# Squares and roots of the second norm issued with the residual, and a broadcast PSUM column as the scan's unused second operand

## Chip, cores, metric

One core of a Trainium2 chip. The metric is the time of one execution of the program in microseconds (us); the time of a kernel is the median of its runs. A profile is one further execution, recorded instruction by instruction.

## What is computed

One layer of a streaming encoder in float32, for a prompt of 2048 frames and a sample of 32 frames with 2048 cached frames. Cut to what matters here:

```python
x = x + rmsnorm(mixer(rmsnorm(x, g_mix_pre)), g_mix_post)   # mixer: stick-breaking attention | SSD, one output projection
x = x + rmsnorm(conv_ffn(rmsnorm(x, g_ffn_pre)), g_ffn_post)

# stick-breaking attention: 8 heads of 64, strictly causal
z = einsum('bqhd,bkhd->bhqk', q, k) * 64 ** -0.5
log_keep  = where(causal, log_sigmoid(-z), 0)
log_after = cumsum(log_keep, reverse=True) - log_keep
w = where(causal, exp(log_sigmoid(z) + log_after), 0)
out = einsum('bhqk,bkhd->bqhd', w, v)
```

The kernel computes `w` without logarithms: beta = sigmoid(z), gam = sigmoid(-z), a running product of gam from the right (a scan), and beta times that product.

## The kernel before

The frames are worked through in four blocks of 512 (the last one of 544, with the sample in it). For each block there are two streams of work.

- **Attention** (`Attention.heads`). Block s has 32 (s + 1) slots, one for 128 queries of one head against 512 keys: 320 slots in all, and 10 more for the sample. A slot is: two score matmuls into the PSUM tile `z` (lines 801 and 805; two buffers, so slot i writes the buffer of slot i-2), two sigmoids on ScalarE (line 652 `beta`, line 656 `gam`), the scan on VectorE into `prow` (line 659), the product (line 664, four of five on GpSimd, one of five on VectorE), four transposes on TensorE into `pt` (line 822), a copy to `wt` (line 825), and after every fourth slot the product with the values into `pa` (line 837). The loop issues the scores of slot i, then some of the other stream (`fill`), then the transposes of slot i-2 (`LOOK = 2`).
- **The rest of the layer** (`Tail.stream`) for the block before, which runs as a generator between the slots. Its matmuls are split into three passes each and go through the helper `dense` (line 124), which fixes their order against the attention's matmuls. In order: the first part of what the block before left over (`owed`, the last two groups of its down projection); the output projection of both halves a and b of the block (`out_units`); `residual(a)`, stepped along with the projection of half b; `residual(b)`; `split` of both halves (`xhi`, `xlo`, the two parts of the next matmuls' input); the rest of `owed`; `root` of both halves; then, for each of 22 units j, `up` (a gate matmul into bank `o`, multiplied by the root `r` on line 984, and an up matmul into bank `u`), and `down` per group of units. The last block's stream runs with no attention beside it.

`residual` takes the root of the mixer's squares (`rstd_narrow`), scales `m`, loads x (DMA, line 930), adds it (line 935, four of eight on GpSimd, four on VectorE), and stores the sum (DMA, line 936). `root` squares that sum, eight pieces per half, and takes the second norm's root `r`. The squares go through one buffer:

```python
    def square(self, sq, x, first):
        if first:
            nc.scalar.activation(sq, x, AF.Square)                         # line 758
        else:
            t = self.tmp.tile([P, 272], F32, name="sqt")[:, : sq.shape[-1]]  # one buffer
            nc.scalar.activation(t, x, AF.Square)                          # line 761
            nc.gpsimd.tensor_tensor(sq, sq, t, op=ALU.add)                 # line 762
```

Each `rstd_narrow` sums the squares with small matmuls into PSUM (line 166), takes the power on VectorE and GpSimd (lines 176 and 184), spreads the result with four small matmuls (line 195) and copies it out on ScalarE (line 201). While attention runs, its two PSUM tiles are taken from the single buffer of bank `u`, which is also that of the up matmuls; tiles of one buffer are handed on in the order in which the program asks for them.

The order of instructions on each engine is fixed at compile time by a planner that takes them roughly in the program's order as it expects them to become ready; on the chip each engine works through its list in order.

Of the kernel before, what the change touches and what calls it, by code (L numbers as in the profile page):

```python
# [23 lines left out]
P = 128  # L24
# [33 lines left out]
def tiles_of(n):  # L58
    return [(0, n)] if n <= 512 else [(0, n // 2), (n // 2, n)]
# [549 lines left out]
class Attention:  # L609
# [38 lines left out]
    def weights_of(self, z, n, prev):  # L648

        nc = self.kn.nc  # L650
        b = self.bp.tile([P, 512], F32, name="beta", bufs=4)
        nc.scalar.activation(b[:, :n], z, AF.Sigmoid, scale=0.125)  # L652
        self.n += 1
        g = self.gam[self.n % 3]
        c0 = 512 - n
        nc.scalar.activation(g[:, c0:512], z, AF.Sigmoid, scale=-0.125)  # L656
        pr = self.pp.tile([P, 513], F32, name="prow", bufs=5)
        back = lambda t: t[:, c0:513][:, ::-1]
        nc.vector.tensor_tensor_scan(  # L659
            back(pr), back(g), back(g), self.kn.ones[:, 0:1] if prev is None else prev,  # L660
            op0=ALU.mult, op1=ALU.bypass,
        )
        eng = nc.vector if self.n % MUL_DVE == 1 else nc.gpsimd
        eng.tensor_tensor(b[:, :n], b[:, :n], pr[:, c0 + 1 : 513], op=ALU.mult)  # L664
        return b, pr[:, c0 : c0 + 1]
# [204 lines left out]
class Tail:  # L870
# [48 lines left out]
    def residual(self, s, half):  # L919

        kn, nc, att = self.kn, self.kn.nc, self.att
        t0 = SBS[s][0]
        c0, c1 = half
        n = c1 - c0
        rm = att.tmp.tile([P, 272], F32, name="rstd")
        kn.rstd_narrow(att.tmp, *kn.bank, [self.msq[:, c0:c1]], n, D, out=rm)
        yield
        for c, m in enumerate(self.m):
            x = (self.late or att.tmp).tile([P, 272], F32, name="xr", bufs=8 if self.late else 2)
            nc.sync.dma_start(x[:, :n], kn.a["xT"][:, c, t0 + c0 : t0 + c1])  # L930
            nc.vector.scalar_tensor_tensor(
                m[:, c0:c1], m[:, c0:c1], kn.col(C_GMIXP + c), rm[:, :n], op0=ALU.mult, op1=ALU.mult
            )
            eng = nc.vector if c % 2 else nc.gpsimd
            eng.tensor_tensor(m[:, c0:c1], m[:, c0:c1], x[:, :n], op=ALU.add)
            nc.sync.dma_start(kn.hS[s][:, c, c0:c1], m[:, c0:c1])
            yield

    def split(self, s, half):
# [14 lines left out]
    def root(self, s, half):  # L954
        kn, nc, att = self.kn, self.kn.nc, self.att
        c0, c1 = half
        if c0 == 0:
            self.r = self.rp.tile([P, 544], F32, name="r", bufs=1)
        for c, m in enumerate(self.m):
            att.square(self.msq[:, c0:c1], m[:, c0:c1], c == 0)  # L960
        col = self.rp.tile([P, 8], F32, name=f"rcol{int(c0 > 0)}")
        kn.rstd_narrow(att.tmp, *kn.bank, [self.msq[:, c0:c1]], c1 - c0, D, out=self.r[:, c0:c1], rcol=col)
        self.cols[s, c0] = col
# [116 lines left out]
    def stream(self, s, cat):  # L1080
        nt = SBS[s][1]
        a, b = (0, nt // 2), (nt // 2, nt)
        owed, self.owed = self.owed or iter(()), None
        yield from islice(owed, 8)
        yield from self.out_units(s, cat, a)
        chain = self.residual(s, a)
        for n, _ in enumerate(self.out_units(s, cat, b)):
            yield
            if n % 4 == 0:
                next(chain, None)  # L1090
        for _ in self.residual(s, b):
            pass
        self.split(s, a)
        self.split(s, b)
        yield from owed
        self.root(s, a)
        self.root(s, b)
        done = iter(())
        if s:
            done = (i for h in (0, SBS[s - 1][1] // 2) for i in self.finish(s - 1, h, h + 256, self.f))  # L1100
        groups = self.GROUPS
        tiles = tiles_of(nt)
        acts = {}
        for g, (j0, n) in enumerate(groups):
            acts[g] = []
            for j in range(j0, j0 + n):
                for i, _ in enumerate(self.up(s, j, acts[g])):
                    yield
                    if j and i % 2:
                        next(done, None)  # L1110
                if j == j0 and g and g < len(groups) - 1:
                    yield from self.down(s, g - 1, acts.pop(g - 1), tiles)
        g = len(groups) - 1

        def last():
            for t in [tiles] if s < NSB - 1 else [[t] for t in tiles]:
                for e in range(2):
                    yield from self.down(s, g - 1 + e, acts[g - 1 + e], t, e == 1)
                if s == NSB - 1:
                    for _ in self.finish(s, *t[0], self.f):  # L1120
                        pass

        self.owed = last()
# [167 lines left out]
```

## Time and profile before

| | |
|---|---|
| median of 3 runs | 3099.98 us (3099.88 to 3104.38) |
| the profiled execution | 3103.09 us, span of its instructions 3101.2 us |
| mean granted TensorE clock | 0.965 |
| busy: TensorE matmul, VectorE, ScalarE, GpSimd | 93%, 55%, 40%, 44% of the span |
| blocks' streams (us from the span's start) | 0 from about 800, 1 from about 1322, 2 from about 1937, 3 from about 2570 |

In the profile's rows PE is TensorE's matmuls, PEld its weight loads, DVE is VectorE, ACT is ScalarE, POOL is GpSimd and SP is the queue that issues DMAs. A group's row gives line, engine, operation, output and inputs, shape and count, then busy us and mean ns of one, then the engine's idle time just before them and what ended it. A row of one line's own view gives the shortest, median and longest duration. In a row of windows "(x" is followed by the number of instructions; PEclk is the granted clock as a share of full speed.

### The profile page before, as it was taken

The page shows a single profiled execution, that of the slowest core. Times are in us where ns is not written, and L with a number is a line of the kernel's source. Part 1 is how long each engine was busy: PE and PEld are TensorE (multiplying, and loading weights), DVE is VectorE, ACT ScalarE, POOL GpSimd, SP SyncE. Part 2 cuts the span into 40 slices and gives each one's busy share as a digit, 9 for nine tenths or more (in the row PEclk, how much of TensorE's full clock was granted, in tenths as well). Part 3 has the DMA queues.
Part 4 walks back from the last instruction along what each step waited for, and adds up shares of the span by engine and source line. Part 5 has one row for each costly group of instructions (what it writes and reads, how often), then busy time and mean ns, then how long its engine had stood idle before and what let it go on. Part 6 is the DMA issues. An engine that isn't in the chain of part 4 may idle for free.

```text
span 3101.2 us, 43193 instructions
## 1 busy us (share of the span) xinstructions
PE 2883.8 (93%) x16175; PEld 2345.9 (76%) x16175; DVE 1690.6 (55%) x2388; ACT 1236.7 (40%) x2504; POOL 1364.9 (44%) x1073
## 2 busy tenths in 40 slices
PE   8999999987879999998899999988999999899996
PEld 6777778865747787785577788855777779799996
DVE  6667667656685643439844443398444324523334
ACT  4344444355565443346633322466433213321111
POOL 4555454355777665547732221376322214511113
PEclk9999999999889999998899999999999999899998
DMA  4545454565655778875264455742645554555455
GB/s 169 175 144 175 138 170 116 165 206 179 234 186 190 246 262 274 277 253 177 89 207 166 165 193 180 251 144 82 211 159 174 201 194 154 175 193 177 165 187 168
DMA packets 234658, 571.57 MB, mean 184 GB/s; under 512 B 49514, under 2 KB 101362, under 8 KB 205906
## 3 DMA queue, kind: packets, MB, share of 16 engines
q1 hardware_dynamic: 234450, 568.81, 55.3%
q8 instruction: 129, 2.11, 0.3%
q14 instruction: 79, 0.65, 0.1%
HBM read 435.22 MB, written 133.50 MB: 183 GB/s over the span
## 4 chain that ended last, share of the span: by engine, by line
PE 62%; DVE 17%; DMA 6%; POOL 6%; ACT 4%; issue 4%; SPq 1%; DVEq 0%; POOLq 0%; ACTq 0%
PE o L124 32%; PE u L124 10%; PE t L124 9%; DVE prow L659 4%; PE pa L837 3%; PE pt L822 2%; POOL beta L664 2%; PE z L801 2%; PE o L365 2%; DVE xc L341 1%; DVE acB L436 1%; POOL msq L762 1%; DMA acB<-acD 1%; DVE f L1072 1%; DVE xc L337 1%
## 5 line engine op out<-in xcount | busy, mean ns | idle before, releaser
L124 PE MATMUL o<-xhi,w 128*128 128x512 f32 (+2 forms) x3968 | 1037.5, 346 | 38.3 <-DMA w<-wS_out 8.8
L124 PEld LDWEIGHTS o<-xhi,w 128*128 128x128 f32 x3968 | 698.2, 192 | 138.8 <-issue 16.9
L124 PE MATMUL o<-xlo,w 128*128 128x512 f32 (+2 forms) x1984 | 684.9, 345 | 9.0 <-DVE xlo L273 4.2
L109 POOL TENSOR_TENSOR w<-wraw,w 128x1024 fp32r<-128x1024 f32 (+2 forms) x156 | 377.0, 2417 | 252.6 <-ACT w L108 237.9
L664 POOL TENSOR_TENSOR beta<-beta,prow 128x512 f32<-128x512 f32 (+3 forms) x264 | 313.5, 1192 | 335.0 <-DVE prow L659 317.5
L124 PEld LDWEIGHTS o<-xlo,w 128*128 128x128 f32 x1984 | 381.0, 192 | 55.5 <-DVE xlo L273 6.0
L1005 POOL TENSOR_TENSOR y<-y,gb 128x512 f32<-128x512 f32 (+1 forms) x88 | 118.3, 1344 | 597.9 <-ACT gb L1004 589.1
L659 DVE TENSOR_TENSOR_SCAN prow<-gam,prow 128x513 f32<-128x513 f32 x200 | 321.0, 1610 | 82.8 <-ACT gam L656 75.2
L124 PE MATMUL u<-xhi,w 128*128 128x512 f32 x1056 | 347.6, 400 | 2.2 <-DVE y L1014 2.1
L124 PE MATMUL o<-ah,w 128*128 128x512 f32 x992 | 334.5, 403 | 9.0 <-DVE f L1051 8.8
L124 PEld LDWEIGHTS u<-xhi,w 128*128 128x128 f32 x1056 | 200.4, 190 | 54.6 <-issue 4.2
L822 PE MATMUL pt<-ident,beta 128*128 128x128 f32 x1088 | 186.4, 293 | 51.8 <-POOL beta L664 37.9
L822 PEld LDWEIGHTS pt<-ident,beta 128*128 128x128 f32 x1088 | 133.7, 148 | 131.3 <-POOL beta L664 61.5
L124 PEld LDWEIGHTS o<-ah,w 128*128 128x128 f32 x992 | 187.7, 189 | 58.6 <-DVE f L1051 11.1
L124 PE MATMUL u<-xlo,w 128*128 128x512 f32 x528 | 210.7, 399 | 0.0
L997 DVE SCALAR_TENSOR_TENSOR y<-gb,cv,y 128x512 f32<-128x512 f32 (+1 forms) x176 | 159.9, 909 | 81.1 <-ACT y L995 78.2
L108 ACT CAST w<-wraw 128x1024 fp32r<-128x1024 f32 (+2 forms) x156 | 155.2, 995 | 118.6 <-PE o L124 49.6
L825 ACT COPY wt<-pt 128x512 f32<-128x512 f32 (+3 forms) x282 | 146.4, 532 | 130.9 <-PE pt L822 127.6
L659 DVE TENSOR_TENSOR_SCAN prow<-gam,ones 128x129 f32<-128x129 f32 (+4 forms) x130 | 142.9, 1109 | 101.9 <-ACT gam L656 101.5
L652 ACT ACTIVATE beta<-z 128x512 f32<-128x512 f32 (+2 forms) x330 | 180.4, 547 | 45.2 <-PE z L801 27.5
L124 PE MATMUL o<-al,w 128*128 128x512 f32 x496 | 197.2, 398 | 0.0
L124 PE MATMUL t<-xhi,w 128*128 128x272 f32 x960 | 190.5, 294 | 4.5 <-DMA w<-wS_up 3.3
(255 smaller groups left out, 4999.0 us busy)
## 6 DMA issues: line engine op xcount, KB each, us to landing
w<-wS_up SPq DMA_DIRECT2D x132, 1024.0 KB, 4.8
w<-wS_dn SPq DMA_DIRECT2D x72, 768.0 KB, 4.8
wS_up<-w SPq DMA_DIRECT2D x44, 1024.0 KB, 4.8
w<-wS_out SPq DMA_DIRECT2D x39, 1024.0 KB, 6.2
wraw<-wup SPq DMA_DIRECT2D x44, 512.0 KB, 5.9
k<-kS SPq DMA_DIRECT2D x80, 256.0 KB, 3.7
wS_dn<-w SPq DMA_DIRECT2D x24, 768.0 KB, 4.5
w<-wS_dn SPq DMA_DIRECT2D x32, 512.0 KB, 4.4
```

The costliest lines, as they stand in the source:

```text
L108: nc.scalar.copy(hi[:, :n, :], raw[:, :n, :])
L109: nc.gpsimd.tensor_tensor(lo[:, :n, :], raw[:, :n, :], hi[:, :n, :].bitcast(F32), op=ALU.subtract)
L124: mm = nc.tensor.matmul(ps[:, : c1 - c0], l[:, k, :], at(r, k0 + k)[:, c0:c1], start=first and i == 0 and k == 0, stop=last and i == 2 and ...
L365: nc.tensor.matmul(vp[h][:q, :260], l[k][:, b * P : b * P + q], rr[:, k, h * 260 : h * 260 + 260], start=i == 0 and k == 0, stop=i == 2 an ...
L652: nc.scalar.activation(b[:, :n], z, AF.Sigmoid, scale=0.125)
L659: nc.vector.tensor_tensor_scan(back(pr), back(g), back(g), self.kn.ones[:, 0:1] if prev is None else prev, op0=ALU.mult, op1=ALU.bypass,)
L664: eng.tensor_tensor(b[:, :n], b[:, :n], pr[:, c0 + 1 : 513], op=ALU.mult)
L822: mm = nc.tensor.transpose(t[:, P * j : P * j + P], w[:, P * j : P * j + P], kn.ident[:])
L825: copy(wt[:, : n // P, P * b : P * b + P], t[:, :n].rearrange("p (i q) -> p i q", q=P))
L837: nc.tensor.matmul(av[DH * (j % 2) : DH * (j % 2) + DH, c0:], v[:, j, :], wt[:, j, c0:], start=kc == s and j < 2, stop=kc == 0 and j > 1,)
L997: nc.vector.scalar_tensor_tensor(y[:, :W], gb[:, i : i + W], kn.col(wc + i), y[:, :W], op0=ALU.mult, op1=ALU.add)
L1005: nc.gpsimd.tensor_tensor(y[:, :W], y[:, :W], t, op=ALU.mult)
```

## The change

Two things are changed. In `weights_of` the scan's second operand, which its operation (`bypass`) passes over, was `gam` itself, read a second time from SBUF; it becomes the first column of the slot's scores in PSUM, repeated along the row. In the tail, each square of the second norm is issued in `residual` behind the store of its piece, in place of `root`; and `root(a)` is issued ahead of `residual(b)`, `root(b)` ahead of the rest of `owed`.

```diff
@@ weights_of
         nc.vector.tensor_tensor_scan(
-            back(pr), back(g), back(g), self.kn.ones[:, 0:1] if prev is None else prev,
+            back(pr), back(g), z[:, 0:1].to_broadcast([P, n + 1]), self.kn.ones[:, 0:1] if prev is None else prev,
             op0=ALU.mult, op1=ALU.bypass,
         )
@@ residual
             eng = nc.vector if c % 2 else nc.gpsimd
             eng.tensor_tensor(m[:, c0:c1], m[:, c0:c1], x[:, :n], op=ALU.add)
             nc.sync.dma_start(kn.hS[s][:, c, c0:c1], m[:, c0:c1])
+            att.square(self.msq[:, c0:c1], m[:, c0:c1], c == 0)
             yield
@@ root
             self.r = self.rp.tile([P, 544], F32, name="r", bufs=1)
-        for c, m in enumerate(self.m):
-            att.square(self.msq[:, c0:c1], m[:, c0:c1], c == 0)
         col = self.rp.tile([P, 8], F32, name=f"rcol{int(c0 > 0)}")
@@ stream
             if n % 4 == 0:
                 next(chain, None)
+        self.root(s, a)
         for _ in self.residual(s, b):
             pass
         self.split(s, a)
         self.split(s, b)
+        self.root(s, b)
         yield from owed
-        self.root(s, a)
-        self.root(s, b)
```

## The prediction

> **What bounds the kernel now.** I read the page's chain first, then the windows along the span, then the matmuls of line 124 in the windows that stand out, then the rows of the lines that the diff touches.
>
> ```profile
> PE 62%; DVE 17%; DMA 6%; POOL 6%; ACT 4%; issue 4%; SPq 1%; DVEq 0%; POOLq 0%; ACTq 0%
> PE o L124 32%; PE u L124 10%; PE t L124 9%; DVE prow L659 4%; PE pa L837 3%; PE pt L822 2%; POOL beta L664 2%; PE z L801 2%; PE o L365 2%; DVE xc L341 1%; DVE acB L436 1%; POOL msq L762 1%; DMA acB<-acD 1%; DVE f L1072 1%; DVE xc L337 1%
> ```
>
> TensorE's work is the bound, so a gain is idle TensorE time taken away. The idle time lies in places:
>
> ```profile
> 905.00:938.00 33.00, 26.06 (x133) 15.79 (x134) 28.59 (x25) 23.88 (x58) 27.32 (x25) 0.90 0.40 128
> 938.00:1320.00 382.00, 378.96 (x1678) 298.76 (x1677) 187.44 (x192) 163.22 (x288) 235.70 (x140) 1.00 0.74 254
> ...
> 1458.00:1516.00 58.00, 47.50 (x225) 27.24 (x224) 48.76 (x41) 42.51 (x98) 50.06 (x42) 0.82 0.22 66
> ...
> 1570.00:1935.00 365.00, 365.00 (x1627) 284.81 (x1627) 158.04 (x191) 111.14 (x227) 92.03 (x77) 1.00 0.52 180
> ...
> 2054.00:2138.00 84.00, 66.06 (x323) 37.07 (x322) 70.12 (x55) 61.62 (x140) 66.83 (x58) 0.88 0.24 69
> ...
> 2222.00:2450.00 228.00, 228.00 (x1024) 174.62 (x1022) 100.80 (x121) 72.69 (x148) 56.13 (x48) 1.00 0.47 162
> ...
> 2651.00:2668.00 17.00, 9.61 (x62) 9.19 (x62) 1.00 (x4) 5.97 (x14) 10.29 (x15) 0.77 0.25 88
> ```
>
> The columns are length, then PE, PEld, DVE, ACT and POOL busy, then the clock. Where attention and the dense matmuls alternate (938, 1570, 2222) TensorE is never idle and its clock is 1.00. In the four short windows it is idle for 6.9, 10.5, 17.9 and 7.4 us, 42.8 together, at clocks of 0.77 to 0.90. The same windows with the dense matmuls of line 124 alone (PE, PEld):
>
> ```profile
> 2054.00:2138.00 84.00, 2.15 (x10) 1.75 (x10) 0.88 0.24 69
> ...
> 1458.00:1516.00 58.00, 0.00 (x0) 0.00 (x0) 0.82 0.22 66
> ...
> 905.00:938.00 33.00, 1.62 (x5) 0.76 (x6) 0.90 0.40 128
> ```
>
> There is next to no dense work in them: TensorE lives on attention alone. Why, the end of the 84 us window shows:
>
> ```profile
> L762 POOL TENSOR_TENSOR msq<-msq,sqt x14: 722/1416/1657, 2074.7 to 2129.0; 128x256 f32<-128x256 f32 x14
> ...
> 2130.49 0.56 PE L166 MATMUL u<-ones,msq 128*128 128x1 f32 x4
> ...
> 2134.81 0.37 ACT L201 COPY r<-u 128x256 f32<-128x256 f32 x1
> ...
> 2136.07 0.40 PE L124 MATMUL u<-xhi,w 128*128 128x512 f32 x1
> ```
>
> Fourteen additions of squares dribble through GpSimd from 2074.7 to 2129, since each passes through one `sqt` buffer and stands behind attention's products; then the root's small matmuls take bank `u`; and 0.9 us after `r` is copied out of `u` at 2135.2 the first up matmul enters that bank. The dense stream stands behind `root(b)`. In the last block, without attention, the same wait is bare:
>
> ```profile
>   POOL msq L762: 10.6, 2
> ```
>
> (Idle before line 166 in 2651:2668, PE and PEld counted apart, so some 5 us.)
>
> **The change part by part.** The sum is made against the profiled execution's 3103.09 us, which is 3.1 above the median of 3099.98.
>
> *Roots earlier.* Per half, eight squares on ACT, seven additions on POOL, and the root (line 166's matmuls, one DVE and one POOL step, line 195's four matmuls, one ACT copy) move ahead of `residual(b)` or of `owed`. No DMA moves; SP's stores of line 936 keep their place in front of the square of the same piece. The pieces are ready here:
>
> ```profile
> L935 DVE TENSOR_TENSOR m<-m,xr x6: 395/686/1305, 2002.7 to 2049.0; 128x256 f32<-128x256 f32 x6
> ```
>
> So the last piece of half b is there at 2050. From the first matmul of line 166 to the end of the copy a root takes 2130.49 to 2135.18, 4.7 us. With one such root now ahead of `residual(b)` (4.7 later) and two squares' lag (about 3 us), `root(b)` ends near 2050 + 4.7 + 3 + 4.7 = 2062, or ten later if the squares still dribble. Of the 81 us from 2054 to 2135 this frees 63 to 73. I take three quarters for all four windows: 0.75 x 42.8 = **-32 us**. Ends: none (another holder of `u` blocks), and all 42.8.
>
> *Clock.* The busy time in these windows runs slow: 26.06 x 0.10 + 47.50 x 0.18 + 66.06 x 0.12 + 9.61 x 0.23 = 21 us lost. I take three quarters again and half of that, since the split's stretch stays as it is: **-8**; ends 0 and -21. [...]
>
> *What the earlier squares and roots displace.* `residual(b)` and so `split(b)` come one root later, since both use the one buffer of `u`: 4.7 us. In blocks 1 to 3 `owed` covers that; block 0 has none, so TensorE waits: **+5**. Ends 0 and +15 (a delay in each of three blocks; squares ahead of products on POOL).
>
> *The scan without its second SBUF read.*
>
> ```profile
> L659 DVE TENSOR_TENSOR_SCAN prow<-gam,prow 128x513 f32<-128x513 f32 x200 | 321.0, 1610 | 82.8 <-ACT gam L656 75.2 <-POOL beta L664 1.9 <-ACT wt L825 0.5
> ...
> L659 DVE TENSOR_TENSOR_SCAN prow<-gam,ones 128x129 f32<-128x129 f32 (+4 forms) x130 | 142.9, 1109 | 101.9 <-ACT gam L656 101.5
> ...
> L659 DVE TENSOR_TENSOR_SCAN prow<-gam,prow x200: 1249/1414/3281, 676.1 to 2452.3; 128x513 f32<-128x513 f32 x100
> ...
> L664 DVE TENSOR_TENSOR beta<-beta,prow x66: 269/694/2465, 632.4 to 2402.9; 128x512 f32<-128x512 f32 x44, 128x384 f32<-128x384 f32 x8, 128x128 f32<-128x128 f32 x7, 128x256 f32<-128x256 f32 x6
> ...
> L1051 DVE TENSOR_TENSOR f<-o,f x152: 658/692/693, 1055.4 to 2526.0; 128x512 f32<-128x512 f32 x152
> ```
>
> The scan of one width takes 1249 to 3281 ns. A DVE product with two SBUF inputs scatters as widely (269 to 2465, though over four widths), while 152 additions with one input in PSUM take 658 to 693, all through the span. So the scatter is that of DVE operations with two SBUF inputs, and the scan loses it. Excess: 200 x (1610 - 1249) = 72 us; the narrower 130 at the same share (361/1610) of 142.9, 32; 104 us of DVE. What of it is on the path:
>
> ```profile
> by line: PE o L124 31.7%; PE u L124 10.3%; PE t L124 9.5%; issue 3.7%; DVE prow L659 3.6%; PE pa L837 2.6%; PE pt L822 2.2%; POOL beta L664 2.1%; PE z L801 2.0%; PE o L365 1.7%; DVE xc L341 1.4%; DVE acB L436 1.2%; POOL msq L762 1.0%; DMA a
> ...
> L664 POOL TENSOR_TENSOR beta<-beta,prow 128x512 f32<-128x512 f32 (+3 forms) x264 | 313.5, 1192 | 335.0 <-DVE prow L659 317.5
> ...
> L664 POOL TENSOR_TENSOR beta<-beta,prow 128x512 f32<-128x512 f32 x188 | 250.9, 1338 | 270.6 <-DVE prow L659 259.9 <-PE o L124 5.3 <-PE pt L822 1.9
> ...
> L664 POOL TENSOR_TENSOR beta<-beta,prow x264: 241/1094/2408, 634.5 to 2453.6; 128x512 f32<-128x512 f32 x94, 128x256 f32<-128x256 f32 x13, 128x128 f32<-128x128 f32 x13, 128x384 f32<-128x384 f32 x11
> ```
>
> 3.6% of 3101 is 112 us of the scans' 464, 24%: **-25 us**. GpSimd's products at full width take 1338 against a median of 1094; 188 x 0.244 = 46 us, half of it the scans' doing, 2.1% (65 us of 313.5, 21%) on the path: **-5**. Ends for both together: 0 (the scan is slowed by something else) and -52 (half on the path). [...]
>
> *The new wait.* The scan now reads `z`, so the score matmul of slot i, which overwrites the buffer of slot i-2, waits for that slot's scan in place of its second sigmoid. Nothing overtakes it on TensorE: dense matmuls are issued behind the scores, transposes behind those, and both sigmoids of slot i wait for it. Where TensorE stands already:
>
> ```profile
>   ACT gam L656: 33.8, 39
> ...
>   ACT gam L656: 26.5, 24
> ...
>   ACT gam L656: 6.3, 13
> ...
>   ACT gam L656: 0.9, 2
> ```
>
> (Idle before line 801: whole span, then 600:960, 1380:1570, 2000:2170.) One of the 39:
>
> ```profile
> 868.03 0.27 ACT L656 ACTIVATE gam<-z 128x128 f32<-128x128 f32 x1
> ...
> 868.35 0.69 PE L801 MATMUL z<-k,qa 128*128 128x384 f32 x1 [4.00 <-ACT gam L656]
> ...
> 869.31 1.96 DVE L659 TENSOR_TENSOR_SCAN prow<-gam,ones 128x129 f32<-128x129 f32 x2
> ...
> 870.70 0.77 POOL L664 TENSOR_TENSOR beta<-beta,prow 128x128 f32<-128x128 f32 x1 [0.36 <-DVE prow L659]
> ```
>
> The scores start 50 ns after the sigmoid; the scan of that slot ends only at about 870.6, 2.3 us later. The wait grows by at least one scan, 1.25 us at full width. The 24 waits in 600:960 stay; of the other 15 half go with the attention-only windows: 31.5 x 1.25 = **+40 us**. Ends: 0 (the transposes would have waited anyway) and 31.5 x 2.3 = +72; a gain is excluded, since a later release lets nothing start earlier. Where slots come every 5 us or so, as in 1570:1935, the scan is long done and the wait is free.
>
> Sum: -32 - 8 + 5 - 25 - 5 + 40 = -25, so 3078 in a profile and **3075 us** as a median.
>
> **The rivals.**
>
> *The new wait decides: slower.* If each of the 31.5 waits costs the 2.3 us of the example (+72) and the scans' relief is half (-15), with the roots as above (-35) the sum is +22: 3122 us. It turns at (35 + 30) / 31.5 = 2.1 us per wait. For it: ScalarE and VectorE sit between one score and the next, and in 600:960 no root is in the way. Against: the example's scan lost 1 us behind other DVE work, and shorter scans catch up.
>
> *The new wait is hidden.* Behind the scores TensorE waits for the product anyway, later than the scan; then the wait only changes its place. With +10 for +40: 3045 us. Against: sigmoids behind the scores start later too.
>
> *The squares stay late.* The planner takes instructions as they get ready; ACT and POOL are busiest just where the squares are to go, and the one `sqt` buffer remains. With a third of the windows freed (-12, no clock) and the rest as above (+10 with the displaced work covered): 3098 us, no change. Against: nothing holds the squares any more behind the group of `owed`.
>
> *The clock follows at once:* 3067 us. For it: 1.00 in every window with alternating work. Against: the stretch of the residual itself stays crowded.
>
> [...]
>
> **How the numbers follow.** Chances: forecast 0.36, new wait decides 0.20, wait hidden 0.14, squares late 0.13, clock at once 0.12, PSUM cost 0.05. A measurement of this kernel tells 0.2%, 6 us, from no change. Faster: 0.33 + 0.14 + 0.04 + 0.12 + 0.04 = 0.67. Slower: 0.18 of the first rival, 0.02 of late squares, 0.01 of the forecast: 0.21. Same: 0.12. Range: 3040 (wait hidden, most of the clock back) to 3118, which leaves out half of the slow rival and a tenth below; the forecast's own range is 3055 to 3093, so that both signs are in the wide one.
>
> **What the changed profile would show.** Roots: dense matmuls of line 124 within 20 us of the split in blocks 1 and 2, clock near 1.00 there, no idle of 5 us before line 166 in the last block. Scan: the full width at 1250 to 1350 in mean and median. Wait: line 801 idle for DVE prow of line 659, some 75 us in place of 33.8 for gam. The prediction is wrong if line 801's idle passes 105 us (33.8 + 72), if the scans' mean stays near 1.6, or if the up matmuls still stand behind the copy of `r` for 50 us.

## The result and the profile after

| | median us (all runs) | ratio to before (95% interval) |
|---|---|---|
| before | 3102.18 (3099.88 to 3107.81, 4 runs) | |
| changed | 3023.51 (3016.09 to 3026.06, 4 runs) | 0.974 (0.9716 to 0.9763) |

The change takes 79 us off. The forecast was 25, and the range ended at 3040. The profiled execution of the changed kernel took 3026.06 us, its span is 3024.3 us. Below, a ratio is turned into microseconds by times 3102. One run of the kernel with the SBUF column below took 5336.78 us at a clock of 0.933 and is left out of its median.

The page's busy times (us, share of the span) of the kernel before, then of the changed kernel, and the changed kernel's chain:

```profile
PE 2883.8 (93%) x16175; PEld 2345.9 (76%) x16175; DVE 1690.6 (55%) x2388; ACT 1236.7 (40%) x2504; POOL 1364.9 (44%) x1073
...
PE 2852.3 (94%) x16175; PEld 2328.8 (77%) x16175; DVE 1560.9 (52%) x2388; ACT 1237.1 (41%) x2504; POOL 1249.5 (41%) x1073
...
PE 72%; DVE 13%; DMA 6%; ACT 3%; issue 3%; POOL 2%; SPq 1%; DVEq 0%; POOLq 0%; ACTq 0%
PE o L124 36%; PE u L124 12%; PE t L124 10%; PE pa L837 4%; PE z L801 3%; PE pt L822 3%; PE o L365 2%; DVE prow L659 2%; DVE xc L341 2%; DVE acB L436 1%; DMA acB<-acD 1%; DMA xr<-xT 1%; DVE x L263 1%; DVE xc L337 1%; POOL beta L664 1%
```

TensorE's share of the chain went from 62% to 72%, VectorE's from 17% to 13%, GpSimd's from 6% to 2%. Of the 76.9 us of span, 31.5 is TensorE being busy for less time with the same 16175 matmuls (2883.8 to 2852.3), and 45.4 is time without a matmul.

The windows of the changed kernel from root(a) to the first up matmul of blocks 1 and 2 and of the last block (length; PE, PEld, DVE, ACT, POOL busy; clock; DMA share, GB/s). Then blocks 1 and 2 from the first copy of the output projection (line 915) to the first up matmul, which is the same tail work in each kernel, in three pairs of rows: before, with the roots alone (the run below) and changed. Then the additions of squares and the first up matmul in block 2 of the changed kernel:

```profile
1388.00:1449.00 61.00, 55.64 (x282) 37.05 (x281) 48.19 (x71) 41.71 (x99) 39.62 (x47) 1.00 0.64 207
1962.00:2023.00 61.00, 56.89 (x298) 38.22 (x294) 51.61 (x72) 42.05 (x99) 34.54 (x42) 1.00 0.63 196
2539.00:2595.00 56.00, 50.39 (x329) 46.39 (x328) 27.39 (x55) 20.70 (x52) 25.46 (x32) 0.97 0.58 193
...
1337.10:1517.40 180.30, 160.67 (x913) 115.97 (x912) 126.51 (x134) 110.25 (x260) 118.70 (x112) 0.91 0.52 169
1951.20:2136.10 184.90, 162.21 (x946) 114.97 (x946) 131.75 (x140) 112.49 (x262) 114.33 (x107) 0.94 0.49 158
...
1341.10:1479.80 138.70, 127.22 (x759) 95.22 (x758) 87.07 (x106) 77.91 (x185) 80.56 (x80) 0.94 0.59 198
1942.40:2072.70 130.30, 121.26 (x746) 92.12 (x745) 87.31 (x107) 71.12 (x169) 70.63 (x71) 0.97 0.61 199
...
1329.10:1448.80 119.70, 114.11 (x722) 88.53 (x720) 69.05 (x99) 71.58 (x172) 65.61 (x77) 1.00 0.69 226
1906.80:2023.30 116.50, 112.12 (x711) 86.97 (x709) 71.36 (x101) 65.35 (x159) 57.55 (x70) 1.00 0.69 224
...
L762 POOL TENSOR_TENSOR msq<-msq,sqt x7: 726/732/922, 1994.6 to 2015.5; 128x256 f32<-128x256 f32 x7
...
2023.27 0.50 PE L124 MATMUL u<-xhi,w 128*128 128x512 f32 x1 [0.50 <-ACT r L201]
```

Where the root's wait was bare of dense work (0.00 and 2.15 us), the windows from root(a) on now hold 26 us of it, most of it the rest of `owed`, which stood ahead of the root before. Over the same tail work, with 72 to 74 us of dense matmuls in each kernel, block 1 takes 120 us in place of 180 and block 2 117 in place of 185, at a clock of 1.00 in place of 0.91 and 0.94. Either part alone shortens block 2's stretch: the roots to 130 us, the scan to 151. In block 2 the last addition starts at 2015 where it was 2129, and the first up matmul at 2023 where it was 2136. It still follows the copy of `r` by half a microsecond, but it is no longer late.

The scans and the products of the changed kernel (times in ns: mean in the rows with "|", shortest, median and longest in the row without):

```profile
L659 DVE TENSOR_TENSOR_SCAN prow<-gam,prow,z 128x513 f32<-128x513 f32 x200 | 255.3, 1277 | 142.6 <-ACT gam L656 136.3 <-POOL sq L762 1.6 <-POOL rcol L184 1.4
L659 DVE TENSOR_TENSOR_SCAN prow<-gam,ones,z 128x129 f32<-128x129 f32 (+4 forms) x130 | 112.0, 867 | 118.7 <-ACT gam L656 106.1 <-PE u L716 11.5 <-PE o L124 0.3
L659 DVE TENSOR_TENSOR_SCAN prow<-gam,prow,z x200: 1250/1281/1285, 682.5 to 2473.7; 128x513 f32<-128x513 f32 x100
L664 POOL TENSOR_TENSOR beta<-beta,prow 128x512 f32<-128x512 f32 x188 | 216.0, 1149 | 331.4 <-DVE prow L659 323.7 <-PE o L124 3.4 <-DVE att L846 1.6
```

The scatter of 1249 to 3281 ns is gone: 1250 to 1285. Attention ends 21 us later than before (the last full scan starts at 2473.7, it was 2452.3) while the kernel ends 77 earlier: more of the dense work now lies under attention.

Idle time of TensorE (us, times): before the scores, line 801, and before the transposes, line 822, of the changed kernel, then before line 822 of the kernel before:

```profile
  DVE prow L659: 86.1, 88
...
  POOL beta L664: 15.8, 21
...
  POOL beta L664: 99.3, 82
```

The new wait is there, 86.1 us where the second sigmoid took 33.8. But at the transposes 99.3 us became 15.8. Together 133 became 102.

### The profile page after: what moved, and what is told of

Read it like the earlier page. It is cut to its first block, busy times and chain, and to the rows that moved or that the text cites. A ratio compares the mean times of both kernels' runs of the same rounds, so it can differ in the third digit from the quotient of the medians.

```text
span 3024.3 us, 43120 instructions
## 1 busy us (share of the span) xinstructions
PE 2852.3 (94%) x16175; PEld 2328.8 (77%) x16175; DVE 1560.9 (52%) x2388; ACT 1237.1 (41%) x2504; POOL 1249.5 (41%) x1073
## 4 chain that ended last, share of the span: by engine, by line
PE 72%; DVE 13%; DMA 6%; ACT 3%; issue 3%; POOL 2%; SPq 1%; DVEq 0%; POOLq 0%; ACTq 0%
PE o L124 36%; PE u L124 12%; PE t L124 10%; PE pa L837 4%; PE z L801 3%; PE pt L822 3%; PE o L365 2%; DVE prow L659 2%; DVE xc L341 2%; DVE acB L436 1%; DMA acB<-acD 1%; DMA xr<-xT 1%; DVE x L263 1%; DVE xc L337 1%; POOL beta L664 1%
## 5 line engine op out<-in xcount | busy, mean ns | idle before, releaser
L109 POOL TENSOR_TENSOR w<-wraw,w 128x1024 fp32r<-128x1024 f32 (+2 forms) x156 | 364.0, 2333 | 255.7 <-ACT w L108 230.9
L664 POOL TENSOR_TENSOR beta<-beta,prow 128x512 f32<-128x512 f32 (+3 forms) x264 | 267.7, 1016 | 412.2 <-DVE prow L659 403.7
L659 DVE TENSOR_TENSOR_SCAN prow<-gam,prow,z 128x513 f32<-128x513 f32 x200 | 255.3, 1277 | 142.6 <-ACT gam L656 136.3
L822 PE MATMUL pt<-ident,beta 128*128 128x128 f32 x1088 | 176.8, 282 | 7.5 <-POOL beta L664 4.4
L656 ACT ACTIVATE gam<-z 128x512 f32<-128x512 f32 (+2 forms) x330 | 179.2, 543 | 0.0
```

The source lines that it names most:

```text
L109: nc.gpsimd.tensor_tensor(lo[:, :n, :], raw[:, :n, :], hi[:, :n, :].bitcast(F32), op=ALU.subtract)
L659: nc.vector.tensor_tensor_scan(back(pr), back(g), z[:, 0:1].to_broadcast([P, n + 1]), self.kn.ones[:, 0:1] if prev is None else prev, op0= ...
L822: mm = nc.tensor.transpose(t[:, P * j : P * j + P], w[:, P * j : P * j + P], kn.ident[:])
```

## The experiments

### The two parts, each alone

Scan alone, on the kernel before (line 660), and roots alone, the changed kernel with that line as it was:

```
-            back(pr), back(g), back(g), ...
+            back(pr), back(g), z[:, 0:1].to_broadcast([P, n + 1]), ...
```

> The kernel before with the scan's second operand alone changed; squares and roots stay where they were. Theory A (the prices of the prediction, added up): -30 for the relief, +40 for the wait, so +10 against before, 3112 us. Theory B (the roots part made nearly all of the 79 us, the scan part is neutral): within 10 us of before, 3092 to 3107. Theory C (the scan part is worth far more than I priced, its wait being hidden): -30 to -50, 3052 to 3072. Scan of full width near 1.28 us in all of them.

> The changed kernel with the scan's second operand put back to the second read of gam in SBUF; only squares and roots are moved. Theory A: -32 - 8 + 5 = -35, 3067 us. Theory B: -65 to -80, 3022 to 3037. Theory C: -30 to -45, 3057 to 3072. If the two parts only pay together (Theory D: the dense work that the roots release makes the wait for z free), scan alone is +10 and roots alone -35 while both are -79.

Scan alone: 3046.70 us, ratio 0.9822 (0.9804 to 0.984), -55 us. Roots alone: 3066.19 us, 0.9886 (0.9865 to 0.9907), -35. Theory A holds for the roots to the microsecond and is wrong by 65 for the scan. Theory C comes closest, though the scan passes its -30 to -50 by 5. The parts add to -90 where both together measure -81, so Theory D falls.

### Which half of the scan's edit

The changed kernel with the second operand a column of a constant SBUF tile; and with the second read of `gam` put back and a one-column copy behind each scan, which keeps the wait and drops the relief:

```
+            back(pr), back(g), self.kn.ones[:, 0:1].to_broadcast([P, n + 1]), ...   # SBUF column
```
```
             back(pr), back(g), back(g), ...
+        zc = self.pp.tile([P, 1], F32, name="zc", bufs=2)
+        nc.vector.tensor_copy(zc[:], z[:, 0:1])
```

> The changed kernel with the scan's second operand a broadcast column of a constant tile in SBUF: no wait of the scores for the scan, and the second operand comes from SBUF again, though always from one address. If the scan is slowed by any second operand from SBUF, its full width stays near 1.6 us, and the time is that of the roots alone (Theory A 3067, B 3025 to 3035). If it is slowed by the bytes that stream, the full width is near 1.28 us, and the time is that of the changed kernel less what the wait for z costs: 3023 - 40 = 2983 by Theory A, 3018 to 3025 if the wait is hidden (B, C).

> The changed kernel with the scan reading gam twice from SBUF as before, and behind each scan a copy of one column of z to a scratch column on VectorE: the wait of the scores for the scan stays, the relief of the scan goes. The copy itself is one small VectorE instruction (330 of some 0.1 us, 24% on the path: about +8). Theory A: roots -35, wait +40, copy +8: 3115 us. If the wait is hidden: the time of the roots alone plus at most 8. Line 801 then idles for VectorE about as long as in the changed kernel (86 us) or longer.

The full scan with the roots alone (the second read of `gam`), with the SBUF column, and with the wait alone, where the copies follow:

```profile
L659 DVE TENSOR_TENSOR_SCAN prow<-gam,prow 128x513 f32<-128x513 f32 x200 | 310.9, 1558 | 113.6 <-ACT gam L656 105.0 <-issue 3.3 <-ACT beta L652 0.9
...
L659 DVE TENSOR_TENSOR_SCAN prow<-gam,prow,ones 128x513 f32<-128x513 f32 x200 | 310.1, 1554 | 111.8 <-ACT gam L656 103.2 <-issue 3.3 <-POOL beta L664 1.6
L659 DVE TENSOR_TENSOR_SCAN prow<-gam,prow,ones x200: 1253/1286/3279, 683.0 to 2525.3; 128x513 f32<-128x513 f32 x100
...
L659 DVE TENSOR_TENSOR_SCAN prow<-gam,prow 128x513 f32<-128x513 f32 x200 | 309.0, 1546 | 144.7 <-ACT gam L656 140.6 <-POOL beta L666 1.0 <-POOL fsq L764 0.4
L664 DVE COPY zc<-z 128x1 f32<-128x1 f32 x330 | 42.5, 129 | 0.0
```

SBUF column: 3067.6 us (four runs), 0.9885 (0.9865 to 0.9906), the time of the roots alone. One column, always the same, costs the scan as much as a stream of 513 (1554 ns in mean against 1558). Wait alone: 3069.73 us, 0.9897 (0.9882 to 0.9912), +3 us over the roots alone (-5 to +12 by the two intervals) with 42.5 us of copies in it. So no cost of the wait shows, where Theory A had put 48 with the copies.

### Why the wait costs nothing

The wait alone on the kernel before (the same two lines of copy); the roots alone with each score held behind the transposes issued before it (no wait):

```
+                if e == 0:
+                    kn.pin(mm)        # first score matmul of a slot, in scores()
```

> The kernel before with nothing but the wait added: behind each scan VectorE copies one column of z, 129 ns each, so the scores two slots on wait for the scan. No relief, squares and roots where they were. Theory W1 (the prediction's price, worked out with TensorE's order as it was): +40 for the wait and 330 x 0.13 x 24% = 10 for the copies, 3154 us. Theory W2 (the planner sees the wait and issues the transposes ahead of the scores that it used to bring forward, so what TensorE waits at the scores it no longer waits at the transposes): 0 to +12, 3104 to 3116 us; scores brought forward over the transposes of three slots back in about 75 of 312 slots in place of 197.

> The kernel with the roots alone moved (3066 us), and each slot's first score matmul held in the program's order behind the transposes of three slots back and the dense work issued with them; no wait for the scan and no relief of it. If the order of TensorE by itself was worth something (W2a: scores brought forward cost as much as the wait does), 3030 to 3055 us. If it is neutral and the wait is simply covered (W2b), 3060 to 3072. If holding the scores back costs (W2c), 3075 to 3110.

Wait on the kernel before: 3093.59 us, 0.9979 (0.9965 to 0.9992): 7 us faster, copies included, and below Theory W2's 0 to +12. Order alone: 3085.22 us, 0.9944 (0.993 to 0.9958), +18 against the roots alone: holding all scores back costs (W2c), so the gain isn't merely that scores come later.

Counted by start times in the traces, the scores of slot j+3 stand ahead of the transposes of slot j in 197 of 308 slots before, in 175 with the roots alone, in 81 with the wait on the kernel before and in 82 in the changed kernel. The planner saw that `z` comes free later and remade TensorE's order. Whether that is the reason takes an order that can't be remade. First one of our own, on the roots alone: scores of slot j+3 ahead of the transposes of j in the same places as there (blocks 1 to 3), with the dense work between them, all held in place:

```
+            upto = i + 1 + (i - LOOK in AHEAD[s])     # AHEAD: the slots j, by block
+            while nxt < min(upto, len(slots)):
+                scores(nxt); nxt += 1                 # then the fill, then turn(i - LOOK)
...                                                    # scores and turn pinned as above
```

> The kernel with the roots alone moved, and the order of scores, dense matmuls and transposes on TensorE written out: in blocks 1 to 3 the scores of slot j+3 stand ahead of the transposes of slot j wherever the planner had put them there (155 of 282 slots), and all three kinds are held to that order. No wait for the scan, no relief. It is the base for the run with the wait. Holding all scores back cost 19 us against the roots alone (3066), so 3065 to 3095 us here.

> The same written-out order, equal for scores, dense matmuls and transposes, and the copy of one column of z behind each scan: the wait with an order that can't give way. Theory W1' (the prediction's price holds for a fixed order and failed because the planner remade the order): +25 to +55 against the fixed order without it (40 for the wait, 10 for the copies). Theory W2b (the wait is covered in any order): 0 to +12.

3077.95 us, 0.9935 (0.9917 to 0.9954), 15 over the roots alone, and with the wait 3077.20 us, 0.9933 (0.9917 to 0.9949): no cost, W1' falls for this order. The idle before the transposes in the kernel with the roots alone and in this order without the wait, then before the scores in this order with the wait, suggest why:

```profile
  POOL beta L664: 56.4, 55
...
  POOL beta L672: 5.5, 3
...
  DVE zc L670: 10.5, 8
```

With dense work standing between scores and transposes throughout, TensorE has next to no attention-only stretch (5.5 us where the roots alone idle 56.4). It was not the order of the kernel before, and so no test of the forecast's price. That order was held next: all scores, dense matmuls, transposes and products with the values of the kernel before, in its compiled order, chained one behind the other. The chain with no other edit was not run; the kernel before, whose order it holds, is the base for both runs. In both traces all 14146 matmuls of these kinds start in the order of before, while the planner still orders the other engines.

```
+    for c, n in re.findall(r"([STVD])(\d*)", ORDER):      # ORDER: the kernel's own sequence
+        for _ in range(int(n or 1)):
+            ins = next(take[c])
+            tc.add_manual_dep(ins, last.name, info, reason="order")
```

> The kernel before with the wait added as in the run with the wait alone (VectorE copies one column of z behind each scan), while scores, dense matmuls, transposes and products with the values are held on TensorE to exactly the order of the kernel before. Theory W1 (the price of +40 was right for that order, and the planner escaped it by remaking the order): 40 + 10 for the copies, 3135 to 3160 us, with some 75 us or more of idle time before the scores and the transposes' 99 us nearly unchanged. Theory W2b (the wait is covered even there, since the transposes behind the scores wait for a later product anyway): 3098 to 3115 us, with the transposes' wait falling about as much as the scores' grows.

> The kernel before with the scan's operand changed (relief and wait) and TensorE held to the order of the kernel before. The same change with the planner free gave 3046.7 us. Theory W1: relief -44 and wait +40, 3090 to 3105 us. Theory W2b: 3045 to 3065 us, and the remade order itself is worth no more than 15.

Wait in the order of before: 3151.68 us, 1.0157 (1.0132 to 1.0183): **+49 us**, where the same wait with the planner free gave -7. Scan's edit in that order: 3076.66 us, 0.9922 (0.9901 to 0.9943), -24 where it gave -55 free. Idle (PE and PEld counted apart) before the scores, the four longest, and before the transposes for GpSimd's product: the wait with the planner free (five rows), and in the old order (five). Then the longest of each for the scan's edit, free and in the old order:

```profile
  DVE zc L664: 59.0, 52
  issue: 45.3, 40
  ACT gam L656: 17.9, 17
  ACT wt L827: 16.2, 13
...
  POOL beta L666: 27.5, 42
...
  DVE zc L687: 82.7, 53
  issue: 53.2, 40
  ACT gam L679: 34.9, 32
  ACT wt L853: 25.6, 22
...
  POOL beta L689: 17.9, 26
...
  DVE prow L659: 93.5, 100
...
  POOL beta L664: 18.9, 32
...
  DVE prow L682: 176.3, 167
...
  POOL beta L687: 10.2, 9
```

For the wait W1 holds: in the old order the price of +40 and 10 for the copies was right (49; the interval is 41 to 57), and with the planner free it is gone. Two expectations beside it were wrong. The transposes' wait, which was to stay at 99, fell to 17.9 there too. And the scan's edit in the old order lies between its two theories (3090 to 3105 and 3045 to 3065): it gains 24, where the forecast's terms for it, -30 and +40, make +10. So the remade order is worth 31 us to the scan's edit, and not all that the forecast missed.

Before the scores the four rows of the wait add to 196 us in the old order and to 138 with the planner free, where a wait of PE and PEld together counts twice. All the time without a matmul is 252.6 us against 212.4, and the matmuls are busy for 2902.5 against 2889.5: together the 53 us between the two profiled executions.

### What the relief is worth, and on which engine

The changed kernel with VectorE's relief given back as plain time (a copy from PSUM behind each scan), and with GpSimd's (a copy ahead of each of its products):

```
+        nc.vector.tensor_copy(zc[:, :k], z[:, :k])        # k = min(n, 144)
```
```
+        if eng is nc.gpsimd:
+            nc.gpsimd.tensor_copy(zc[:, : n // 2], pr[:, c0 + 1 : c0 + 1 + n // 2])
```

> The changed kernel with VectorE's relief taken back as plain time: behind each scan a copy of 144 columns from z's PSUM bank, some 0.28 us by 129 ns for one column and 681 for 512, which is what a full scan lost (1558 to 1277 ns), 330 x 0.28 = 94 us in all. GpSimd stays relieved. By the 24% of the prediction +23, 3046 us. If VectorE's time is most of what the relief gave (46 us between the wait alone and the changed kernel): +35 to +46, 3058 to 3070. If GpSimd's relief is most of it: +0 to +15, 3023 to 3038.

> The changed kernel with GpSimd's relief taken back as plain time: ahead of each of GpSimd's 264 products, and behind the scan, GpSimd copies half of the scan's row to a scratch tile, some 0.3 us, 80 us in all (GpSimd was busy 93 us longer with the roots alone). VectorE's scans stay at 1.28 us. By the 21% of the prediction +17, 3040 us. If GpSimd's time is most of what the relief gave: +35 to +46, 3058 to 3070; if VectorE's is: +0 to +15, 3023 to 3038.

```profile
L665 DVE COPY zc<-z 128x144 f32<-128x144 f32 (+1 forms) x330 | 92.0, 279 | 0.0
...
L666 POOL COPY zc<-prow 128x256 f32<-128x256 f32 (+3 forms) x264 | 112.3, 425 | 253.5 <-DVE prow L659 247.7 <-PE o L124 2.0 <-DVE rn_v L186 1.8
```

VectorE: 3047.65 us, 0.9828 (0.9815 to 0.9842), 27 us over the changed kernel for 92.0 us of copies: 0.30 per microsecond, where the prediction had 24%. GpSimd: 3070.29 us, 0.9909 (0.9894 to 0.9924), 52 us for 112.3: 0.47, where it had 21%. The second is an upper price, since each copy delays its product by its full length. Both engines' time counts. The two prices add to 79 us, more than the whole relief (49 us between the wait alone and the changed kernel, copies included), so they can't be added, and how the relief divides between the engines stays open.

If GpSimd's microsecond is the dearer one, products should move to VectorE (`MUL_DVE = 5` to 3 and to 2):

> The changed kernel with one product in three on VectorE in place of one in five: 44 products leave GpSimd (44 x 1.1 = 48 us) and load VectorE with 44 x 0.8 = 35 us. By the padded runs a microsecond of GpSimd is worth up to 47/112 = 0.42 and one of VectorE 24/92 = 0.26: -20 + 9 = -11, 3012 us. If GpSimd's weight is only that of its products' delay (0.17): -8 + 9 = +1, 3024 us.

> The changed kernel with one product in two on VectorE in place of one in five (one in three gave 3011 us, 8 below a kernel like the changed one on that chip): 99 products leave GpSimd in all. If GpSimd's time goes on being the dearer, -15 to -20, 3003 to 3009; if VectorE, which then carries 80 us more, takes over, 3015 to 3030.

One in three: 3011.22 us, 0.9719 (0.9704 to 0.9734), 8 us under the run of the next section, which is the changed kernel in time and ran on the same chip; the prices had said -11. One in two: 3015.68 us, 0.9722 (0.9697 to 0.9746): no further gain, as was expected if VectorE's load takes over; whether it does stays open.

### What of the roots part counts

Both roots behind the rest of `owed` again, the squares left with the pieces of the residual:

```
-        self.root(s, a)                  # ahead of residual(b)
...
         yield from owed
+        self.root(s, a)
+        self.root(s, b)
```

> The changed kernel with both roots put back behind the rest of owed; the squares stay with the residual's pieces. If the squares' late additions were what held the roots, as the prediction's rows of line 762 suggest, most of the roots' 23 us (3046.7 for the scan alone less 3023.5) stays: 3023 to 3032. If it is the roots' own place in the program (bank u is handed on in that order): 3038 to 3048.

3019.40 us, 0.974 (0.9726 to 0.9755): the changed kernel's time. Beside the scan's change, the earlier squares are all of the roots' gain; the roots' own place moves nothing that these runs resolve.

Two buffers for the squares, `name="sqt", bufs=2` in `square`: with one product in three on VectorE, alone on the changed kernel, and alone on the kernel before:

> The changed kernel with one product in three on VectorE and two buffers for the squares (sqt) in place of one. ScalarE's squares wait 47 us for that buffer in the changed kernel, on no path that ends last by the result of moving the roots: 3008 to 3014, no change against one in three alone. If the buffer still holds the roots: 2995 to 3006.

> The changed kernel with two buffers for the squares (sqt) and the products left at one in five on VectorE. With one product in three on VectorE the second buffer took 20 us off (3011 to 2991). If the two edits add, 3023 - 20 = 3003 us. If the second buffer only pays once GpSimd is freed of products, 3015 to 3023.

> The kernel before with two buffers for the squares and nothing else. If the single buffer was what made the squares dribble from 2074 to 2129 us and so held root(b), this takes back much of what the roots part gave (35 us): 3065 to 3080. If the squares are late because they stand behind the rest of owed in the program, a second buffer alone changes little: 3092 to 3104.

| second buffer on | median us | ratio to before |
|---|---|---|
| changed kernel, one product in three | 2990.95 | 0.9645 (0.9623 to 0.9668) |
| changed kernel | 2981.92 | 0.9617 (0.9596 to 0.9638) |
| kernel before | 3053.48 | 0.9842 (0.9824 to 0.986) |

All three expectations were too small. A second buffer of 272 columns is worth 38 us on the changed kernel and 49 on the kernel before, more than the 35 of moving squares and roots. Idle of ScalarE before its squares, before and with the second buffer on the kernel before; then the additions in block 2 there:

```profile
L761 ACT ACTIVATE sqt<-m 128x256 f32<-128x256 f32 (+1 forms) x112 | 47.7, 426 | 41.5 <-POOL msq L762 37.3 <-POOL fsq L762 0.8
L761 ACT ACTIVATE sqt<-f 128x256 f32<-128x256 f32 (+1 forms) x56 | 23.8, 426 | 43.8 <-POOL fsq L762 36.0 <-DVE f L1051 7.4 <-DVE rn_v L186 0.4
...
L761 ACT ACTIVATE sqt<-m 128x256 f32<-128x256 f32 (+1 forms) x112 | 47.9, 430 | 28.8 <-POOL msq L762 22.7 <-POOL fsq L762 3.0
L761 ACT ACTIVATE sqt<-f 128x256 f32<-128x256 f32 (+1 forms) x56 | 22.3, 418 | 18.2 <-POOL fsq L762 9.0 <-DVE f L1051 9.0
L762 POOL TENSOR_TENSOR msq<-msq,sqt x14: 716/1190/1652, 2032.8 to 2063.9; 128x256 f32<-128x256 f32 x14
```

The fourteen additions take 31 us in place of 54, and ScalarE's wait for the buffer falls from 73 to 32 us; its sigmoids and copies stand in the same queue behind those squares. How much of the 49 us comes by the roots and how much by that queue was not separated.

The changed kernel with the second buffer is the fastest of all; one product in three adds nothing to it.

## Why the prediction was wrong

| term | predicted | measured | from |
|---|---|---|---|
| roots, clock, displaced work | -32 - 8 + 5 = -35 | -35 (-42 to -29) | roots alone |
| the scan's relief | -25 - 5 = -30 | -36 | scan alone less wait on before, -49, of which the copies' 42.5 us x 0.30 = 13; changed less wait alone: the same |
| the new wait | +40 | -10 to -20 | wait alone on either base, +3 and -7, less the same 13 |
| sum | -25 | -81 to -91 | measured together: -81 (-88 to -74) |

- **The wait is the step that failed**, 50 to 60 us of it where the whole miss is 56. The sentence "Nothing overtakes it on TensorE" took the order in the trace of before as given, and "a gain is excluded" rested on that. The planner makes the order anew from the dependences, and the edit added one for each slot: scores that had been issued ahead of three-slot-old transposes went back in 115 places (197 to 82). Held to the old order the wait alone costs +49 with the copies, 36 without, close to the forecast.
- **Adding the wait to the relief failed too.** In the old order the scan's whole edit gave -24 where the terms make +10. Of the 65 us that the forecast missed on the scan's edit (+10 to -55), 31 go with the remade order and 34 are there in the old order as well. Whether the relief is worth more there, or the wait costs less behind a scan that is 0.28 us shorter, was not separated and stays open.
- **The sign named as decisive**, line 801 idle for the scan, was 86.1 against "some 75" and under 105. It came true while the cost it stood for did not.
- **Better than free.** Why the wait with the planner free is a gain stays open. The new order may be better than the old one; but with the wait alone on the kernel before GpSimd was also busy for 33 us less (1364.9 to 1331.8), and the full scans took 1546 ns in place of 1610.
- **The rival "the wait is hidden"** (3045) was right in that the idle moves from the transposes to the scores. That alone did not hide it, since in the old order the transposes' idle went as well (17.9) and the wait still cost. Priced at +10, it ended 22 us short.
- **Relief.** Within its ends (0 to -52), 6 short. VectorE's share on the path (24%) measured 30%. GpSimd's was sized too small: with the scan's edit alone its busy time fell by 115 us (1364.9 to 1249.4), where the forecast took half of 46, since the additions of line 762 sped up (976 to 765 ns) as well as the products (1338 to 1135); and a microsecond of it costs up to 0.47. That the scan is slowed by its second SBUF read was right: 1277 ns mean without it, 1558 with it (roots alone).
- **Roots.** The sum was right, to the microsecond in part by luck, and the reason half right. Dense work fills the stretch in blocks 1 and 2, and line 166 idles 0.8 us for `msq`. But root(a)'s place, named for the 4.7 us of displaced work, counts for nothing, so no run shows the +5; the squares do all. And the one `sqt` buffer, named as a cause of the dribble, was then left in the price of a rival alone; it is worth more than the move.
- **Clock.** The 1.00 in both windows is that of the two parts together. With the roots alone the stretch of the same tail work stands at 0.94 and 0.97, where it was 0.91 and 0.94: part of the loss came back, as forecast, and the scan's edit brought the rest. In the two traces the granted clock is 0.50 or 1.00 at each moment. Leaving out the end of the span, it is 0.50 in 38 stretches of 3.4 to 10.2 us before (198 us together) and in 24 of 3.4 to 13.7 us in the changed kernel (126 us), and TensorE's matmuls are busy for 86% or more of the last 3.4 us of each. So a few us of busy matmuls bring it back, which speaks for the rival "clock at once": its 3067 is the forecast with all of the 16 us (three quarters of 21) in place of 8.
- **PSUM cost.** No run shows one, though 0.05 of the chances went to it: the median scan is 1281 ns with the column in PSUM and 1286 with the one in SBUF, the shortest 1250 and 1253, with the other input in SBUF in both.
- **Two readings.** The 1094 ns for GpSimd's product is a median over four widths; at full width alone it is 1097. In the rival "the squares stay late" a third of the 42.8 us is 14, not 12. Neither changes the sum.

## What to carry to other kernels

Where a planner orders instructions at compile time, price a new dependence for a remade order, not for the one in the trace of before: here the same wait cost +49 us in the old order and -7 in the new, copies included. Count the SBUF operands of a scan beside GpSimd work, used or not (1667 ns here with a second one, 1276 without), and move one to PSUM if the tile is there anyway (55 us here, with the wait that this brings). When a chain of small steps dribbles through one buffer, try the second buffer before moving the steps: it was worth 49 us against 35.

## What the runs showed of the hardware

- An SBUF operand that the scan passes over and that is one column repeated slowed it as much as 513 different ones: 1554 ns mean against 1558 with the second read of `gam` (roots alone), and 1277 with the column in PSUM. The second read slowed the scan only beside GpSimd: of the 232 full scans of the kernel before, the 78 with no GpSimd instruction beside them took 1282 ns in mean and at most 1287, the 97 with GpSimd busy for over 80% of their time took 1667, and the 57 between took 1871. In the changed kernel 72 scans with as much of GpSimd beside them took 1276.
- The relief goes both ways. With the scan's edit alone GpSimd's full-width products fell from 1338 to 1135 ns and its additions of squares from 976 to 765 (the two rows: the kernel before, scan alone), with no change to either:

```profile
L762 POOL TENSOR_TENSOR msq<-msq,sqt 128x256 f32<-128x256 f32 (+1 forms) x112 | 109.4, 976 | 71.7 <-ACT sqt L761 71.5
...
L762 POOL TENSOR_TENSOR msq<-msq,sqt 128x256 f32<-128x256 f32 (+1 forms) x112 | 85.7, 765 | 83.8 <-ACT sqt L761 83.5
```
